# Delta rule in a streaming trunk: the first inverse correction from 16-bit copies, and the decay columns as the exponential's bias

## Chip, core and metric

The kernel runs on one core of a Trainium2 chip. The metric is the device time in microseconds of one execution. The core's engines are TensorE (PE in the profile; PEld is its weight load), VectorE (DVE), ScalarE (ACT), GpSimd (POOL) and SyncE (SP), which here issues all the DMAs.

## What is computed

One layer of a hybrid trunk, for a prompt of 2048 tokens and 64 further tokens of a running stream. Half of the mixing width is a gated delta rule with 4 heads of 128, the other half a multi-scale pool; both go through one output projection, and a SwiGLU FFN follows. The delta rule is evaluated in chunks. For one head and one chunk, cut to what matters here:

```
G     = cumsum(g)                                   # log decay
gamma = exp(where(lower_incl, G[:, None] - G[None, :], -inf))
Lm    = where(lower_strict, (k * beta) @ k.T * gamma, 0)
T     = inverse(eye + Lm)                           # triangular
u, w  = T @ (v * beta), T @ (k * beta * exp(G))
qk    = (q @ k.T) * gamma
v_new = u - w @ S;  o = (q * exp(G)) @ S + qk @ v_new
S     = S * exp(G[-1]) + (k * exp(G[-1] - G)).T @ v_new
```

The inputs are 32-bit; the large matrix products are made of split operands (a high and a low part) in a faster format.

## The kernel before, in words

**Order of the work.** The function hybrid_kernel does not call the engines. It calls a class Machine, which notes each operation with its operands, and issues all of them at the end, in an order that a list scheduler finds (issue, pick and run): per engine, the operation of the lowest rank that is ready. It knows costs of each operation and latencies between engines. On TensorE it keeps operations of three kinds: "r" (float32r, the dense products), "f" (32-bit) and "h" (16-bit); f and h go ahead of r when they are ready, and may be held for a moment (HOLD) while r goes on. Each engine then works through its own list in order. The order on an engine is thus a result of the operations and of the table of costs: a change of a few operations moves others.

**The stages.** First four blocks of 512 prompt tokens (block 0 has the 64 stream tokens too). A block j has: the norm (norm_apply), the input projection (project; tiles pp, from h and the weights wsp), the decay rows (rows), four heads (head_project, then a Head), four pool groups and, one block later, the output projection (out_proj; tiles pz). Then the FFN in three blocks of 704 tokens (gate_up, down, down_strassen), from about 970 us. The weights are 32-bit in memory and split into two float32r parts by ACT and DVE.

**rows** makes, for all heads of a block, the cumulated log decay: Ghl holds it by rows in a high and a low float32r part; a small matmul into the tile pc turns it into columns, one for each chunk and head, and ACT takes their exponential into EC.

**A front** (class Front, all) treats two chunks of 128 tokens of one head; there are 32 for the prompt and one (h is None) for the stream tokens. Its steps, each on the next engine:
- TensorE turns the keys (ptk), ACT scales them (ktl) and takes norms (kn).
- rowmm writes the row G, the same in all partitions, into the PSUM tile gb; ACT takes its exponential (EG, in the tile TV32).
- Into the same gb TensorE adds the mask (negm, 16-bit, 0 or -1e30) and, by negmm, minus the column G: two float32r matmuls with seln as the moving operand. ACT takes exp of all 256 columns at once: Gam is gamma for two chunks.
- GpSimd takes the identity off (U, in the tile Gst), TensorE makes the products gr, DVE multiplies: U is Lm plus the strict part's scale, Gam becomes qk.
- Seven levels double the block size of the inverse in 16 bits. Each has GpSimd's mask (Um), two matmuls py, ACT's copy Yt, four matmuls pt and DVE's difference (TV). The last writes 32 bits: T and V, the inverse and its transpose.
- Two Newton corrections in 32 bits: GpSimd makes F = I - T, TensorE pf = U T, DVE F = F - pf; then px0 = F V, T = V + px0 on DVE; then px1 = F T, X = V + px1.
- TensorE turns the values (ptv), ACT scales them (vtk).

A front's tiles are taken by slot (NLEV = 3), and its operations are ranked early (BOOST). Head.prompt then goes through the chunks in order: pk, rhs, vn, po and the new state Sp.

The lines that the change touches are in Front.negmm, Front.all and rows. Almost every operation is recorded at one line, 278, where issue calls the engine; so in the profile operations are known by their tiles. In these names digits that belong to buffers are left out: gb_p is the tile gb of a prompt's front.

Of the kernel before, what the change touches and what calls it, by code (L numbers as in the profile page):

```python
# [9 lines left out]
F16 = mybir.dt.float16  # L10
BF16 = mybir.dt.bfloat16
F32 = mybir.dt.float32
F32R = mybir.dt.float32r
AF = mybir.ActivationFunctionType
# [4 lines left out]
P = 128  # L19
# [3 lines left out]
DEC = 64  # L23
NTOK = SEQ + DEC
C = 128
NF = 22
EPS = 1e-6
NH = 4
# [9 lines left out]
SO = PB[0] + 3  # L38
# [315 lines left out]
def hybrid_kernel(ctx, tc, a, o):  # L354
    nc = machine = Machine(tc.nc)
    act = nc.scalar.activation
# [6 lines left out]
    def cost(n, dt):  # L363
        clock["pe"] += n * (1.67e-3 if dt == F32 else 0.427e-3) + 0.005

    def mm(out, lhsT, rhs, start, stop, **kw):
        nc.tensor.matmul(out, lhsT, rhs, start=start, stop=stop, **kw)
        n = 1
        for d in out.shape[1:]:
            n *= d  # L370
        cost(n, rhs.dtype)
# [55 lines left out]
    def pool(name, where=ctx, early=False, behind=False, **kw):  # L427
        return Pool(machine, where.enter_context(tc.tile_pool(name=name, bufs=1, **kw)), early, behind)
# [7 lines left out]
    cp1, gp = pool("cp1", p1, True), pool("gp", p1, True)  # L436
# [49 lines left out]
    for j in range(NBLK):  # L486
        win = [("win", m) for m in range(21)]
        at = 5 + 4 * OUT_AFTER
# [324 lines left out]
    B = Block(0)  # L813
# [5 lines left out]
    at = 0  # L819
# [18 lines left out]
    seln = cp1.tile([P, 4, 1], F32R, tag="seln", name="seln")  # L838
# [5 lines left out]
    negm = cp1.tile([P, P], BF16, tag="negm", name="negm")  # L844
    nc.vector.tensor_copy(negm, lm_f[:, 7])

    negm2 = cp1.tile([P, P], BF16, tag="negm2", name="negm2")
# [4 lines left out]
    idbf = cp1.tile([P, P], BF16, tag="idbf", name="idbf")  # L852
# [9 lines left out]
    def bc(t, nch, n):  # L862
        return t.unsqueeze(1).to_broadcast([t.shape[0], nch, n])
# [4 lines left out]
    class Front:  # L868
# [39 lines left out]
        def negmm(self, ps):  # L908

            G = self.B.Ghl  # L910
            if self.h is None:
                for h in range(NH):
                    mm(ps[:, h * DEC : (h + 1) * DEC], G[:, SO : SO + P], seln[:, h, :].to_broadcast([P, DEC]),
                       start=False, stop=False)
            else:
                for c in range(2):
                    at = self.off + c * C
                    mm(ps[:, c * C : (c + 1) * C], G[:, at : at + C], seln[:, self.h, :].to_broadcast([P, C]),
                       start=False, stop=c == 1, skip_group_check=True)

        def all(self):
            tag, chunk = self.tag, self.chunk
            two = lambda ps: ps[:, : 2 * C].rearrange("p (c n) -> p c n", n=C)
            gt = lambda shape, dt, t, bufs, n="": gp.tile(shape, dt, tag=t, name=f"{t.split('_')[0]}{n}_{tag}", bufs=bufs)
            slot = self.i % NLEV
            lev = lambda dt, t, n="", shape=[P, 2, C], bufs=1: gt(shape, dt, f"{t}_{slot}", bufs, n)
# [9 lines left out]
            for c in range(2):  # L936
# [8 lines left out]
            gb = self.ps(f"gb_{tag}")  # L945
# [5 lines left out]
            nc.gpsimd.tensor_copy(EL, EG.rearrange("p c n -> p (c n)").rearrange("p (e n) -> p e n", n=n)[:, :, n - 1 : n])  # L951
            Qd = self.Qd = gt([P, 2, C], F32, "Qd", NOUT)
            tt(Qd, self.Yqk[:, 0, self.off : self.off + 2 * C].rearrange("p (c n) -> p c n", n=C), EG, ALU.mult)
            dd = gb if self.h is not None else self.ps(f"dd_{tag}")
            mm(dd[:, : 2 * C], idbf, bc(negm2 if self.h is None else negm, 2, C), start=dd is not gb, stop=False,
               skip_group_check=dd is gb)
            self.negmm(dd)
            if dd is not gb:
                self.rowmm(dd, False)
            Gam = self.QKG = gt([P, 2, C], F32, "Gam", NOUT)  # L960
            act(Gam, two(dd), AF.Exp)
            U = lev(F32, "Gst")
            nc.gpsimd.tensor_tensor(out=U, in0=Gam, in1=bc(ident, 2, C), op=ALU.subtract)
            yield LAT_G
            ps = self.ps(f"gr_{tag}")
# [36 lines left out]
            T, V = TV32[:, 0], TV32[:, 1]  # L1002
            F = lev(F32, "F")
            nc.gpsimd.tensor_tensor(out=F, in0=bc(ident, 2, C), in1=T, op=ALU.subtract)
            pf = self.ps(f"pf_{tag}")
            for c in range(2):
                mm(pf[:, c * C : (c + 1) * C], U[:, c], T[:, c], start=True, stop=True)
            tt(F, F, two(pf), ALU.subtract)
            yield LAT_F
            px = self.ps(f"px0_{tag}")  # L1010
            for c in range(2):
                mm(px[:, c * C : (c + 1) * C], F[:, c], V[:, c], start=True, stop=True)
            tt(T, V, two(px), ALU.add)
            yield LAT_D
            yield self.before(NX, "used")
# [1 line left out]
            px = self.ps(f"px1_{tag}")  # L1017
# [119 lines left out]
    def rows(B, pab):  # L1137

        j, YW, nch = B.j, B.YW, B.nch
        Ghl = B.Ghl = gp.tile([P, SO + P], F32R, tag="Ghl", name=f"Ghl{j}", bufs=2)  # L1140
        EC = B.EC = gp.tile([P, 4, 12], F32, tag="EC", name=f"EC{j}", bufs=2)
# [29 lines left out]
        pc = psg(f"pc{j}")  # L1171
        for c, (lo, n) in enumerate(chunks):
            mm(pc[:n, c * 12 : c * 12 + 12], Rt[:, lo : lo + n], sel12, start=True, stop=True)
        act(EC[:, :nch, :], pc[:, : 12 * nch].rearrange("p (c t) -> p c t", t=12), AF.Exp)
        if B.dec:

            ECs = B.ECs = cp1.tile([P, 3, 2], F32, tag="ECs", name="ECs")
            for i in range(2):
                t = slice(i * DEC, (i + 1) * DEC)
# [173 lines left out]
    for j in range(NBLK):  # L1353
# [34 lines left out]
        prev, B = B, (nxt if nxt is not None else B)  # L1388
# [23 lines left out]
    for k in (4, 5, 6, 7, 0, 1, 2, 3):  # L1412
        t = wpool.tile([P, 512], F32, tag="xc", name=f"od{k}", bufs=XBUFS["xc"])
# [22 lines left out]
    for nm in FH[3:]:  # L1436
        t = f2.tile([P, 4, 2, N2], F32R, tag=f"h{nm}", name=f"hB{nm}")
# [172 lines left out]
    for op in order:  # L1610
        b = op[1]
        if op[0] == "gu":
            f = op[2]
# [6 lines left out]
            if plain(b, gi):  # L1620
                if f == groups[gi][0] or f == groups[gi][0] + 2:
                    two = opool.tile([P, 2, 2, TB2], F32R, tag="op", name=f"h3l{f}_{b}", bufs=2)
# [8 lines left out]
        else:  # L1631
            f0, G = groups[op[2]]
# [25 lines left out]
NY, NLEV, NOUT, NX = 3, 3, 3, 2  # L1658
# [128 lines left out]
```

## Time and profile before

| | |
|---|---|
| median of 3 runs | 2384.84 us (2381.84 to 2387.46) |
| the profiled execution | 2383.12 us |
| its span, first to last instruction | 2380.5 us |
| mean granted TensorE clock | 0.997 |
| DMA | 540.57 MB, mean 227 GB/s |

The time of an execution is a little more than the span, by 2.6 us here. A row of a timeline has its start, its length and the engine, then the tiles (written tile, arrow, read tiles), the shape and the number of instructions merged. Matmuls overlap, so a length is not what one costs; the distance between two starts is. A 32-bit matmul of the program leaves two records, a float32r or 16-bit one leaves one. Idle time stands in brackets or after a bar, with the engine that ended it.

### The profile page before, as it was taken

How to read it: one execution, taken by the hardware profiler on the slowest of the kernel's cores; microseconds unless marked ns; L12 is line 12 of the kernel's file. 1: busy time of each engine (PE TensorE's matmuls, PEld its weight loads, DVE VectorE, ACT ScalarE, POOL GpSimd, SP SyncE). 2: the span in 40 equal slices, each digit the busy share in tenths (PEclk: the TensorE clock that was granted, in tenths of full speed). 3: DMA queues.
4: the chain of work that ended last, by engine and by line, in shares of the span. 5: the costliest groups of instructions: out<-in, count | busy, mean ns of one | idle time of the engine just before them, and what ended most of it. 6: DMA issues, size and time to landing. Idle time of an engine off the chain costs nothing.

```text
span 2380.5 us, 41651 instructions
## 1 busy us (share of the span) xinstructions
PE 2344.3 (98%) x14823; PEld 2184.7 (92%) x14823; DVE 1674.3 (70%) x2943; ACT 1215.7 (51%) x2738; POOL 967.2 (41%) x1130
## 2 busy tenths in 40 slices
PE   9999999999999999999999999999999999999998
PEld 8999798777887778899999999999999999999998
DVE  7999875785577686787776883767566657646466
ACT  6666654564456565574454654553334554425334
POOL 1656452554346662264332536353233464202211
PEclk9999999999999999999999999999999999999999
DMA  7643566445555565998876678887855697565763
GB/s 267 224 165 134 189 228 217 146 165 190 176 182 172 162 195 166 311 373 324 312 282 240 257 270 271 295 287 248 283 189 175 201 348 247 193 227 193 260 209 114
DMA packets 228384, 540.57 MB, mean 227 GB/s; under 512 B 28240, under 2 KB 86608, under 8 KB 228176
## 3 DMA queue, kind: packets, MB, share of 16 engines
q1 hardware_dynamic: 228176, 537.92, 66.2%
q8 instruction: 116, 1.90, 0.3%
q14 instruction: 92, 0.75, 0.1%
HBM read 389.41 MB, written 148.41 MB: 226 GB/s over the span
## 4 chain that ended last, share of the span: by engine, by line
PE 81%; DVE 9%; ACT 3%; DMA 3%; issue 2%; SPq 1%; POOL 1%; DVEq 0%; POOLq 0%; ACTq 0%
PE px L278 19%; PE pp L278 14%; PE pz L278 11%; PE py L278 9%; PE d L278 8%; PE dx L278 5%; PE dy L278 3%; PE pk_p L278 2%; PE pt_p L278 1%; PE dz L278 1%; PE gr_p L278 1%; PE px_p L278 1%; DVE Yqk L278 1%; PE py_p L278 1%; ACT E L278 1%
## 5 line engine op out<-in xcount | busy, mean ns | idle before, releaser
L278 PE MATMUL pp<-h,wsp 128*128 128x512 f32 (+1 forms) x2480 | 562.1, 366 | 2.0 <-DVE h L278 1.7
L278 PEld LDWEIGHTS pp<-h,wsp 128*128 128x128 f32 x2480 | 402.3, 190 | 49.8 <-DVE h L278 2.6
L278 POOL TENSOR_TENSOR Um_p<-Gst_p,lmask 128x256 f16<-128x256 f32 x224 | 178.2, 809 | 109.6 <-PE py_p L278 80.9
L278 PE MATMUL pz<-op,wsp 128*128 128x512 f32 (+1 forms) x960 | 216.8, 366 | 3.4 <-ACT op L278 2.9
L278 PE MATMUL d<-h3l,wsd 128*128 128x352 f32 x1248 | 201.3, 322 | 0.2 <-DVE h3l L278 0.2
L278 PEld LDWEIGHTS d<-h3l,wsd 128*128 128x128 f32 x1248 | 199.1, 188 | 1.2 <-DVE h3l L278 0.7
L278 PEld LDWEIGHTS pz<-op,wsp 128*128 128x128 f32 x960 | 155.9, 190 | 23.2 <-ACT op L278 3.4
L278 DVE TENSOR_TENSOR TV_p<-TV_p,pt_p 128x512 f16<-128x512 f16 (+1 forms) x192 | 128.5, 681 | 48.7 <-PE pt_p L278 43.4
L278 PE MATMUL px<-hA,ws 128*128 128x352 f32 x792 | 141.2, 322 | 0.6 <-DMA ws<-g 0.6
L278 PE MATMUL pz<-hB,ws 128*128 128x352 f32 x792 | 139.6, 322 | 0.6 <-DMA ws<-g 0.6
L278 PE MATMUL px<-hBT,ws 128*128 128x352 f32 x792 | 137.8, 322 | 2.1 <-DVE u L278 2.1
L278 PE MATMUL px<-hBT,wsS 128*128 128x352 f32 x792 | 137.7, 322 | 2.0 <-ACT g L278 1.9
L278 PE MATMUL py<-hB,wsS 128*128 128x352 f32 x792 | 139.2, 322 | 0.1
L278 PE MATMUL px<-hA,wsS 128*128 128x352 f32 x792 | 137.4, 322 | 0.9 <-ACT g L278 0.9
L278 PE MATMUL py<-hA,wsS 128*128 128x352 f32 x792 | 137.1, 322 | 0.0
L278 ACT ACTIVATE hr<-g 128x352 f32<-128x352 f32 x132 | 65.6, 497 | 133.4 <-DVE g L278 133.4
L278 PEld LDWEIGHTS px<-hBT,wsS 128*128 128x128 f32 x792 | 128.2, 188 | 2.8 <-ACT g L278 2.8
L278 PEld LDWEIGHTS px<-hBT,ws 128*128 128x128 f32 x792 | 128.0, 188 | 2.9 <-DVE u L278 2.7
L278 PEld LDWEIGHTS px<-hA,ws 128*128 128x128 f32 x792 | 128.9, 188 | 1.0 <-DMA ws<-g 0.9
L278 PEld LDWEIGHTS pz<-hB,ws 128*128 128x128 f32 x792 | 128.6, 188 | 0.8 <-ACT hB L278 0.8
L278 PEld LDWEIGHTS px<-hA,wsS 128*128 128x128 f32 x792 | 128.3, 188 | 1.2 <-ACT g L278 1.1
L278 PEld LDWEIGHTS py<-hB,wsS 128*128 128x128 f32 x792 | 128.6, 188 | 0.4 <-ACT u L278 0.4
(686 smaller groups left out, 5354.5 us busy)
## 6 DMA issues: line engine op xcount, KB each, us to landing
wsS<-gS SPq DMA_DIRECT2D x176, 512.0 KB, 4.7
ws<-g SPq DMA_DIRECT2D x132, 512.0 KB, 4.6
wsp<-wnd SPq DMA_DIRECT2D x126, 512.0 KB, 3.3
gS<-wsS SPq DMA_DIRECT2D x88, 512.0 KB, 5.6
g<-ws SPq DMA_DIRECT2D x66, 512.0 KB, 5.5
wnd<-wsp SPq DMA_DIRECT2D x42, 512.0 KB, 4.5
xd<-x2d SPq DMA_DIRECT2D x96, 176.0 KB, 4.0
wrd<-in_wd_dram SPq DMA_DIRECT2D x48, 256.0 KB, 4.7
```

The costliest lines, as they stand in the source:

```text
L278: getattr(getattr(self.nc, op.eng), name)(*args, **kw)
```

## The change

The decay columns: negmm is left to the stream's front. A prompt's front now ends the group in gb with the mask, and ACT takes the exponential of each chunk alone, with minus the column G as its bias, one number for each partition. This column is a new tile NG, which rows writes from the same PSUM tile pc as EC, with factor -1.

The first correction: ACT copies V and F to a 16-bit tile VF (it takes the slot's buffer TV0, free by then; in the order it is called TV0w), and px0 is made from the copies by 16-bit matmuls. The second correction is still in 32 bits, from F and T.

```
         def negmm(self, ps):
 
             G = self.B.Ghl
-            if self.h is None:
-                for h in range(NH):
-                    mm(ps[:, h * DEC : (h + 1) * DEC], G[:, SO : SO + P], seln[:, h, :].to_broadcast([P, DEC]),
-                       start=False, stop=False)
-            else:
-                for c in range(2):
-                    at = self.off + c * C
-                    mm(ps[:, c * C : (c + 1) * C], G[:, at : at + C], seln[:, self.h, :].to_broadcast([P, C]),
-                       start=False, stop=c == 1, skip_group_check=True)
+            for h in range(NH):
+                mm(ps[:, h * DEC : (h + 1) * DEC], G[:, SO : SO + P], seln[:, h, :].to_broadcast([P, DEC]),
+                   start=False, stop=False)
...
-            dd = gb if self.h is not None else self.ps(f"dd_{tag}")
-            mm(dd[:, : 2 * C], idbf, bc(negm2 if self.h is None else negm, 2, C), start=dd is not gb, stop=False,
-               skip_group_check=dd is gb)
-            self.negmm(dd)
-            if dd is not gb:
+            Gam = self.QKG = gt([P, 2, C], F32, "Gam", NOUT)
+            if self.h is None:
+                dd = self.ps(f"dd_{tag}")
+                mm(dd[:, : 2 * C], idbf, bc(negm2, 2, C), start=True, stop=False)
+                self.negmm(dd)
                 self.rowmm(dd, False)
-            Gam = self.QKG = gt([P, 2, C], F32, "Gam", NOUT)
-            act(Gam, two(dd), AF.Exp)
+                act(Gam, two(dd), AF.Exp)
+            else:
+                mm(gb[:, : 2 * C], idbf, bc(negm, 2, C), start=False, stop=True, skip_group_check=True)
+                for c in range(2):
+                    act(Gam[:, c], two(gb)[:, c], AF.Exp, bias=self.B.NG[:, self.c0 + c, self.h : self.h + 1])
...
             tt(F, F, two(pf), ALU.subtract)
+            VF = lev(F16, "TV0", "w", [P, 2, 2, C])
+            nc.scalar.copy(VF[:, 0], V)
+            nc.scalar.copy(VF[:, 1], F)
             yield LAT_F
             px = self.ps(f"px0_{tag}")
             for c in range(2):
-                mm(px[:, c * C : (c + 1) * C], F[:, c], V[:, c], start=True, stop=True)
+                mm(px[:, c * C : (c + 1) * C], VF[:, 1, c], VF[:, 0, c], start=True, stop=True)
             tt(T, V, two(px), ALU.add)
...
-        act(EC[:, :nch, :], pc[:, : 12 * nch].rearrange("p (c t) -> p c t", t=12), AF.Exp)
+        pcs = pc[:, : 12 * nch].rearrange("p (c t) -> p c t", t=12)
+        act(EC[:, :nch, :], pcs, AF.Exp)
+        NG = B.NG = gp.tile([P, 4, NH], F32, tag="NG", name=f"NG{j}", bufs=2)
+        act(NG[:, :nch], pcs[:, :, :NH], AF.Copy, scale=-1.0)
```

Where instructions stand now is shown at three places. In the names p_3_1 is the second front of head 3 (of the block at hand); h_2 is the normed input of block 2, pp_20 an input projection's tile; a number at the end only tells buffers apart.

TensorE in the third block, where the last front's decay is made; before:

```order
L278 LDWEIGHTS idbf
L278 MATMUL gb_p_3_1_2175<-negm,idbf 128x256
L278 MATMUL pk_p_2_1_2171<-rhs_p_2_1_2172,X_p_2_1_2123 128x128
L278 MATMUL gb_p_3_1_2175<-seln,Ghl_1500 128x128 x2
L278 MATMUL pp_20_0_2049<-h_2_1444,wsp_79_1996 128x512 x4
```

The same place now:

```order
L278 LDWEIGHTS idbf
L278 MATMUL gb_p_3_1_2202<-negm,idbf 128x256
L278 MATMUL pk_p_2_1_2198<-rhs_p_2_1_2199,X_p_2_1_2149 128x128
L278 MATMUL pp_19_0_2072<-h_2_1459,wsp_78_2000 128x512 x5
L278 LDWEIGHTS TV_p_3_0_2164
```

The pair of seln between the 32-bit step pk and the dense matmuls is gone; the dense matmuls now follow pk itself.

TensorE in the second block, from pf to px0 of front p_3_0; before:

```order
L278 MATMUL pf_p_3_0_1536<-TV_p_3_0_1380,Gst_p_3_0_1385 128x128 x2
L278 MATMUL pp_20_0_1401<-h_1_774,wsp_50_1349 128x512 x7
L278 MATMUL px_p_3_0_1537<-TV_p_3_0_1380,F_p_3_0_1535 128x128 x2
L278 LDWEIGHTS Um_p_3_1_1575
L278 MATMUL py_p_3_1_1577<-TV_p_3_1_1554,Um_p_3_1_1575 128x128
```

The same place now:

```order
L278 MATMUL pf_p_3_0_1554<-TV_p_3_0_1395,Gst_p_3_0_1400 128x128 x2
L278 MATMUL pk_p_2_1_1558<-Sp,Yqk_2_1232 128x128
L278 MATMUL po_p_2__1500<-Qd_p_2_1_1331,Sp 128x128
L278 MATMUL pp_20_0_1414<-h_1_762,wsp_50_1363 128x512 x3
L278 MATMUL pp_19_0_1413<-h_1_763,wsp_49_1341 128x512 x4
L278 LDWEIGHTS TV0w_p_3_0_1555
L278 MATMUL px_p_3_0_1556<-TV0w_p_3_0_1555 128x128
```

Between pf and px0 there were seven dense matmuls, and there are seven and two steps of the preceding head; px0 reads only the copies.

ACT in the second block, around the copies of the same front; before:

```order
L278 ACTIVATE Gam_p_3_1_1528<-gb_p_3_1_1525 128x256
L278 CAST Yt_p_3_0_1499<-py_p_3_0_1498 128x256
L278 CAST op_1_1216<-pd_1_1405 128x512
L278 CAST Yt_p_3_0_1517<-py_p_3_0_1516 128x256
L278 ACTIVATE vn_p_2_1_1545<-pk_p_2_1_1539,kn_p_2_1_1310 128x128
L278 CAST Yt_p_3_1_1556<-py_p_3_1_1555 128x256
L278 CAST h_2_1444<-xb_1088_1446 128x512
```

The same place now:

```order
L278 CAST Yt_p_3_0_1535<-py_p_3_0_1534 128x256
L278 ACTIVATE Gam_p_3_1_1546<-gb_p_3_1_1543,NG_832 128x128 x2
L278 ACTIVATE vn_p_2_1_1552<-pk_p_2_1_1539,kn_p_2_1_1319 128x128
L278 CAST TV0w_p_3_0_1555<-TV_p_3_0_1395 128x256
L278 CAST TV0w_p_3_0_1555<-F_p_3_0_1553 128x256
L278 CAST h_2_1459<-xb_1088_1461 128x512
```

The exponential of the other front is in two parts with NG as an operand, and the two copies stand together ahead of the next block's h.

## Prediction

> **What bounds the kernel now.** I read the page first, then a table of the span cut into stages, then the waits of the TensorE, and last its timeline inside one stage. The page gives the span and the share of the busiest engine:
>
> ```profile
> span 2380.5 us, 41651 instructions
> ...
> PE 2344.3 (98%) x14823; PEld 2184.7 (92%) x14823; DVE 1674.3 (70%) x2943; ACT 1215.7 (51%) x2738; POOL 967.2 (41%) x1130
> ```
>
> The TensorE has 36 us without a matmul. All that the change touches runs in the four token blocks of the delta stage, before about 970 us. This is the table by stage; the first two numbers of a row are its ends and its length, and each engine's busy time follows with its count of instructions:
>
> ```profile
> core 0: us, PE busy (x) PEld busy (x) DVE busy (x) ACT busy (x) POOL busy (x), PEclk, DMA share, GB/s
> ...
> 60.00:245.00 185.00, 182.53 (x1491) 169.76 (x1490) 174.71 (x351) 117.58 (x302) 114.49 (x163) 1.00 0.53 179
> 245.00:480.00 235.00, 232.53 (x1514) 197.89 (x1515) 165.83 (x302) 128.40 (x315) 98.39 (x137) 1.00 0.57 192
> 480.00:715.00 235.00, 234.65 (x1397) 188.33 (x1397) 157.26 (x277) 122.67 (x306) 104.39 (x146) 1.00 0.53 178
> 715.00:970.00 255.00, 247.14 (x1464) 199.30 (x1463) 191.63 (x338) 143.12 (x358) 131.60 (x169) 0.99 0.57 177
> ...
> 1080.00:2381.00 1301.00, 1283.70 (x7992) 1275.84 (x7990) 855.20 (x1443) 591.84 (x1212) 459.84 (x446) 1.00 0.71 245
> ```
>
> Between 60 and 970 us the TensorE lacks 185+235+235+255 less 182.53+232.53+234.65+247.14, which is 13.2 us in 910. ACT is busy 52 to 64 per cent of each of these stages, DVE 67 to 94. The TensorE's waits on steps of the fronts (a front is the chain that inverts two chunks of one head) are short and few; the columns are the total, the number of waits and the longest:
>
> ```profile
> PE pt_p L278 <- ACT Yt_p L278: 1.4, 2, 0.9
> ...
> PE ptv_p L278 <- DVE X_p L278: 0.7, 1, 0.7
> PE py_p L278 <- DVE TV_p L278: 0.7, 2, 0.5
> ...
> PE px_p L278 <- DVE TV_p L278: 0.4, 1, 0.4
> ```
>
> 33 fronts with some twenty dependent steps each cost 3.2 us of waits in these four rows together. The dense matmuls (pp, the input projection; pz, the output projection) fill the time in which a front's step is on another engine. So in this stage time is what the TensorE has to issue, and a matmul taken from it is worth its distance to the next start, not its recorded duration (the records overlap). These are distances in the second block; a row is start, length, instructions:
>
> ```profile
> 437.81 0.29 PE L278 MATMUL py_p<-TV_p,Um_p 128*128 128x128 f16 x2
> 437.94 0.66 PE L278 MATMUL pf_p<-TV_p,Gst_p 128*128 128x128 f32 x4
> ...
> 439.39 0.28 PE L278 MATMUL gb_p<-negm,idbf 128*128 128x256 bf16 x1
> 439.51 0.28 PE L278 MATMUL pt_p<-Yt_p,TV_p 128*128 128x128 f16 x2
> 439.62 0.28 PE L278 MATMUL pt_p<-TV_p,Yt_p 128*128 128x128 f16 x2
> 439.71 0.41 PE L278 MATMUL gb_p<-seln,Ghl 128*128 128x128 f32 x2
> 439.96 0.45 PE L278 MATMUL pp<-h,wsp 128*128 128x512 f32 x1
> 440.24 0.61 PE L278 MATMUL px_p<-TV_p,F_p 128*128 128x128 f32 x4
> 440.69 1.04 PE L278 MATMUL gr_p<-Yqk 128*128 128x256 f32 x4
> 441.56 0.61 PE L278 MATMUL pf_p<-TV_p,Gst_p 128*128 128x128 f32 x4
> 442.01 0.61 PE L278 MATMUL px_p<-TV_p,F_p 128*128 128x128 f32 x4
> 442.37 1.87 PE L278 MATMUL pp<-h,wsp 128*128 128x512 f32 x7
> 444.09 0.28 PE L278 MATMUL py_p<-id,Um_p 128*128 128x128 f16 x2
> 444.21 0.66 PE L278 MATMUL px_p<-TV_p,F_p 128*128 128x128 f32 x4
> 444.71 0.38 PE L278 MATMUL ptv_p<-consts,Yvz 128*128 128x128 f32 x2
> ...
> 445.86 0.29 PE L278 MATMUL py_p<-TV_p,Um_p 128*128 128x128 f16 x2
> 445.98 0.66 PE L278 MATMUL px_p<-TV_p,F_p 128*128 128x128 f32 x4
> 446.48 0.39 PE L278 MATMUL pk_p<-rhs_p,X_p 128*128 128x128 f32 x2
> ```
>
> A step of two chunks in 32-bit (px, shown as x4, since such a matmul leaves two records) keeps the TensorE for 0.45, 0.36, 0.50 and 0.50 us, a mean of 0.45. The 16-bit step of the same size (py and pt, x2) keeps it for 0.13, 0.11, 0.09, 0.12 and 0.12, a mean of 0.11. The pair of column matmuls (seln) keeps it for 0.25. One price is hidden: what it costs to come back to the dense matmuls. Their pace when nothing interrupts is in these rows:
>
> ```profile
> 614.20 0.39 PE L278 MATMUL os_p__1942<-osh_p__1943,onesr 128*128 128x512 f32 x1
> 614.43 0.62 PE L278 MATMUL pp<-h,wsp 128*128 128x512 f32 x2
> 614.90 0.40 PE L278 MATMUL os_p__1942<-osl_p__1944,onesr 128*128 128x512 f32 x1
> 615.13 15.59 PE L278 MATMUL pp<-h,wsp 128*128 128x512 f32 x68
> 630.57 0.60 PE L278 MATMUL ptk_p<-consts,Yqk 128*128 128x128 f32 x4
> ```
>
> From 615.13 to 630.57 are 68 matmuls, 0.227 us each. The seven at 442.37, which follow a 32-bit step, take 1.72 where 7 x 0.227 is 1.59: 0.13 for the return. The two at 614.43, which follow a matmul of the same number format as theirs (float32r), take 0.47 where 0.45 is due: 0.02; the one at 439.96, after seln, also float32r, 0.28: 0.05.
>
> **The change, part by part.** *The first correction from 16-bit copies.* 33 fronts replace one 32-bit step by a 16-bit one: 33 x (0.45 - 0.11) = 11.2 us off the TensorE. By the extremes of the rows it is 33 x (0.36 - 0.13) = 7.6 to 33 x (0.50 - 0.09) = 13.5; I take the means, since the step falls beside both kinds of neighbours.
>
> The Trainium skill, page "TensorE: Matmul & The Clock Gate", section "Back-to-back issue gap", gives about 81 ns for each matmul with its weight load in a sustained stream of 128 columns. By it the 16-bit step would keep the TensorE for 0.16 us and the saving would be 33 x 0.29 = 9.6; the trace has 0.11 for just this shape, and that is used.
>
> *The column matmuls.* 32 fronts lose the pair of seln, 32 x 0.25 = 8.0 us. The mask (negm) stays and now ends the group; at 0.12 before another 16-bit step it is neither cheaper nor dearer.
>
> *The order of the TensorE.* The scheduler writes another order, and it interrupts the dense matmuls more often. Counted along both orders up to the first FFN matmul, the dense matmuls are resumed 401 times after a 32-bit or 16-bit step and 88 times after float32r before, and 456 and 66 times after. The pair of seln used to be a cheap way back, and pieces that stood in one group now stand apart. At 0.12 and 0.03 that is 55 x 0.12 - 22 x 0.03 = 6.0 us given back. Its bounds are nothing (if the gaps of the dense matmuls hide it) and 55 x 0.13 = 7.2.
>
> *ACT.* These rows price what ACT gets (busy time, then mean ns of one):
>
> ```profile
> L278 ACT ACTIVATE vn_p<-pk_p,kn_p 128x128 f32<-128x128 f32 x64 | 23.6, 368 | 45.8 <-PE pk_p L278 45.7
> ...
> L278 ACT ACTIVATE Gam_p<-gb_p 128x256 f32<-128x256 f32 x32 | 12.2, 385 | 1.6 <-PE gb_p L278 1.4
> ...
> L278 ACT CAST wsd<-wrd 128x256 fp32r<-128x256 f32 x24 | 9.7, 402 | 18.2 <-PE py L278 10.5 <-PE px L278 4.2 <-PE pz L278 3.5
> ```
>
> The copies are of the last kind: 66 x 0.40 = 26.5 us. The decay exponential becomes two of the first kind, with a column as an operand: 32 x (2 x 0.37 - 0.385) = 11.4. The negated column, once a block, is small: four at 0.37 at most, 1.5. Together 39 us, which takes ACT from 52-64 per cent of the stages to about 56-69. On the path to the end I cost it at nothing: the dense matmuls hide it. The front itself gets longer by one copy, 0.40 and a handover, so about 0.45 us from F to px0 (V's copy is done while pf runs); against that the exponential no longer waits for the seln pair. If the cover is gone in every front it costs 33 x 0.45 = 14.9 us, which is more than the gain; the four waits above say that cover is nearly always there.
>
> *Not touched.* No DMA, no DVE and no GpSimd instruction is added. The order of the TensorE from the first FFN blocks on is the same, so the 1301 us from 1080 us on stay, and shift.
>
> The sum: -11.2 - 8.0 + 6.0 = -13.2 us. The profiled execution took 2383.1, 1.7 under the median of the runs, 2384.84; the sum gives 2369.9 against the one and 2371.6 against the other. I predict 2371.
>
> **Rivals.** *The chain paces the stage, not the TensorE* (no change). For it: weight loads fill only 188.33 of the 235 us from 480 on, and DVE is at 94 per cent in the first block. The Trainium skill, page "Perfetto Trace Analysis", section "Identifying the Most-Contended Engine", calls matmul busy time a poor measure of headroom and takes the busy share of weight loads instead; by that rule there is a fifth of headroom in this stage and the removed matmuls would buy little. Against it: 0.35 us without a matmul in that stage, and dense matmuls at an even 0.227. Then what is saved turns into waits, and the time stays within 4.8 us of the median, 2380 to 2385. Chance 0.08.
>
> *ACT's queue stands* (slower). ACT works in order. The copy of F waits for the TensorE (pf) and DVE; four copies of the next block's h, vn and Yt are queued behind it, and the TensorE needs them. If the copy stands at the head too early by 1.0 us a front and the TensorE has nothing left to fill with, 33 us come on top: 2371 + 33 = 2404. It decides from 13.2/33 = 0.40 us a front for no gain, and from (13.2+4.8)/33 = 0.55 for slower by 0.2 per cent. Against it: the waits of Yt, same engine and same kind of place, reach the TensorE with 1.4 us in the whole run. Chance 0.05.
>
> *The weight load sets the pace of the 16-bit step* (a smaller gain). A weight load of this kind takes 98 ns:
>
> ```profile
> L278 PEld LDWEIGHTS <-TV_p x384: 95/98/102, 66.4 to 939.6; 128*128 128x128 f16 x192
> ```
>
> If it isn't hidden, the new step keeps the TensorE for 0.20 and not 0.11, 33 x 0.09 = 3.0 us less gain: 2374. The Trainium skill, page "TensorE: Matmul & The Clock Gate", section "LDWEIGHTS (loading the stationary operand)", gives columns / 1.2, so 107 ns, in the same direction. Against it: the rows of py and pt, with such loads, stand 0.09 to 0.13 apart. Chance 0.04, within the range.
>
> That the change does nothing is excluded by the order: seln is gone and the 16-bit step is there.
>
> **How the numbers follow.** The forecast has 0.83. Its best case is 13.5 + 8.0 with no price for returns, 21.5 us: 2361.6. Its worst has 7.6 + 8.0 - 7.2 = 8.4, and the copy's latency showing in a third of the fronts, 11 x 0.45 = 5.0: 3.4 left, 2379.7 against the profiled run and 2381.4 against the median. So the range is 2362 to 2381. About 0.2 per cent, 4.8 us, is what a measurement of this kernel can tell from no change, so faster means under 2380. Faster has 0.83 and 0.04 less a little for the worst case, 0.86; same 0.09; slower 0.05.
>
> **What would show it.** Right: no gb_p<-seln group; the 16-bit px step 0.09 to 0.13 us from the next start; the delta stage shorter by 10 to 16 us and the FFN stage equal; ACT up by about 39 us; waits of the TensorE on the new copies of a few us at most. Wrong: a row of TensorE waits on these copies, on Yt, h or wsp of more than 5 us; the delta stage as long as before with the TensorE less busy; or a new order with more returns than counted.

## The result, and the profile after

| | before | after |
|---|---|---|
| median | 2383.43 us (15 runs, 2380.63 to 2387.46) | 2378.36 us (15 runs, 2374.22 to 2382.42) |
| ratio to before, 95% interval | | 0.9976 [0.9968, 0.9984] |
| span of the profiled execution | 2380.5 us | 2376.5 us |
| mean granted TensorE clock | 0.997 | 0.995 |

The changed kernel is faster by 0.24%, 5.7 us by the ratio (the two medians lie 5.1 apart, the two profiled spans 4.0), where 13.2 were forecast: the right direction, less than half of the size. The page of the changed kernel, its span and engines:

```profile
span 2376.5 us, 41477 instructions
...
PE 2334.8 (98%) x14693; PEld 2168.0 (91%) x14693; DVE 1670.3 (70%) x2943; ACT 1245.3 (52%) x2840; POOL 967.8 (41%) x1130
```

The TensorE is 9.5 us less busy than the 2344.3 of before, yet the span is only 4.0 shorter. It now stands still for 41.7 us, where it was 36.2. The same table by stage as before:

```profile
60.00:245.00 185.00, 180.18 (x1454) 165.67 (x1452) 171.70 (x349) 124.79 (x327) 114.09 (x162) 0.99 0.53 180
245.00:480.00 235.00, 231.72 (x1498) 195.11 (x1499) 165.22 (x306) 137.16 (x343) 97.19 (x138) 1.00 0.58 194
480.00:715.00 235.00, 234.46 (x1400) 187.97 (x1399) 158.59 (x285) 131.62 (x333) 109.35 (x151) 1.00 0.54 181
715.00:970.00 255.00, 246.95 (x1427) 193.85 (x1426) 198.84 (x339) 153.94 (x389) 129.69 (x165) 0.99 0.60 187
```

Between 60 and 970 us the TensorE lacks 4.82 + 3.28 + 0.54 + 8.05 = 16.7 us, where it lacked 13.2. ACT's share of these stages rose to 56 to 67 per cent, where 56 to 69 were forecast; over the whole span ACT is busy 29.6 us more, not 39. What its new instructions cost, from the groups of ACT:

```profile
L278 ACT ACTIVATE Gam_p<-gb_p,NG 128x128 f32<-128x128 f32 x64 | 20.1, 375 | 1.8 <-PE gb_p L278 1.7
L278 ACT CAST TV0w_p<-F_p 128x256 f16<-128x256 f32 x32 | 13.1, 411 | 14.2 <-DVE F_p L278 14.0
L278 ACT CAST TV0w_p<-TV_p 128x256 f16<-128x256 f32 x32 | 13.0, 406 | 11.8 <-DVE TV_p L278 11.8
```

375 and 411 ns stand against 370 and 400 forecast. ACT's records overlap, and busy time counts an overlap once: the 64 exponentials are busy for 20.1 us, where 64 x 0.375 is 24.0. The new 16-bit step in the second block, from the timeline (start, length, instructions):

```profile
443.54 0.28 PE L278 MATMUL px_p<-TV0w_p 128*128 128x128 f16 x2
443.63 0.95 PE L278 MATMUL pp<-h,wsp 128*128 128x512 f32 x3
444.42 0.29 PE L278 MATMUL px_p<-TV0w_p 128*128 128x128 f16 x2
444.51 0.94 PE L278 MATMUL pp<-h,wsp 128*128 128x512 f32 x3
```

From its start to the next are 0.09 us in these two places. Over the 32 fronts of the prompt the mean is 0.11, as forecast. The weight load does not set its pace; that would be 0.20.

**Where the time went.** The table is worked out from the traces. For each matmul it takes the distance to the next one's start, without the time in which no matmul ran, sums it by kind up to the first FFN matmul (px from hA), and puts the time without a matmul in a column of its own. The levels are the 16-bit steps with the mask; float32r are the seln pairs, the norms and row sums; time at half clock is inside the kinds. The last column runs from the first FFN matmul to the end of the span. Each row is one profiled execution; that of e2 is 5.8 us over the median of its runs, the others lie within 2.

| kernel | dense | 32-bit steps | 16-bit px | float32r | levels | no matmul | FFN begins at | to the end |
|---|---|---|---|---|---|---|---|---|
| before | 705.8 | 169.5 | - | 33.5 | 70.3 | 16.3 | 996.5 | 1384.0 |
| after | 712.0 | 156.2 | 3.6 | 24.9 | 71.4 | 19.6 | 988.7 | 1387.8 |
| e1 columns | 704.0 | 169.7 | - | 25.2 | 70.3 | 16.7 | 987.1 | 1383.2 |
| e2 copies | 711.8 | 157.7 | 3.7 | 33.1 | 71.1 | 21.0 | 999.5 | 1390.8 |
| e6 F by DVE | 707.7 | 159.0 | 3.4 | 25.3 | 69.7 | 14.8 | 981.0 | 1382.9 |
| e8 hold | 703.1 | 157.2 | 3.5 | 24.9 | 70.4 | 14.9 | 975.0 | 1387.9 |
| e9 pools | 709.0 | 155.8 | 3.7 | 25.2 | 71.5 | 16.0 | 982.3 | 1383.1 |
| e13 hold and pools | 699.6 | 156.3 | 3.5 | 25.1 | 69.5 | 8.7 | 963.8 | 1385.9 |

After against before: the first correction -13.3 + 3.6 = -9.7, the columns -8.6, the dense matmuls with their returns +6.2. Those are the three terms of the forecast (-11.2, -8.0, +6.0). Then come three that it did not have: +1.1 in the levels, +3.3 without a matmul, and +3.8 in the FFN. Together they are 8.2 us.

Two places, the end of the delta stage and the start of the FFN, have longer waits than before. The waits of the TensorE in the changed kernel (total, number, longest):

```profile
PE px L278 <- ACT g L278: 5.3, 4, 2.7
PE py_p L278 <- DVE TV_p L278: 3.6, 5, 1.4
PE pz L278 <- ACT op L278: 3.0, 2, 2.3
```

And two of these rows before:

```profile
PE pz L278 <- ACT op L278: 2.9, 2, 2.2
PE px L278 <- ACT g L278: 2.7, 3, 1.4
```

The levels' py waited 0.7 on TV before and 3.6 now, so the four rows of waits that the prediction showed grew from 3.2 to 5.1 us. The copies needn't be the reason: in e1, which has none, py waits 2.8. The waits of pz on op are no longer in total than before, but they now stand elsewhere: the longest of before ended at 886 us, and there the changed kernel waits 2.15 us for DVE's wsp instead. The end of the delta stage, first before:

```profile
960.30 1.02 PE L278 MATMUL os_p__2961<-osq_p__2960,ones 128*128 128x512 f32 x2
960.75 8.76 PE L278 MATMUL pz<-op,wsp 128*128 128x512 f32 x35
969.68 27.03 PE L278 MATMUL pz<-op,wsp 128*128 128x512 f32 x118 [0.17 <-ACT wsp L278]
```

And the same place after:

```profile
951.96 1.02 PE L278 MATMUL os_p__2998<-osq_p__2997,ones 128*128 128x512 f32 x2
952.42 2.88 PE L278 MATMUL pz<-op,wsp 128*128 128x512 f32 x10
957.58 31.31 PE L278 MATMUL pz<-op,wsp 128*128 128x512 f32 x129 [2.28 <-ACT op L278]
```

os is the sum of squares with which the last head of the last block is normed. Its output op follows some 5 us later, and the rest of pz needs it. Before, 35 other pz were left to fill that time; now there are 10, and 2.28 us stand empty. The stock of dense work is fixed by now, and the order had used more of it between the earlier steps: 139 pz are left behind os, where 153 were.

The second place is the start of the FFN. The TensorE's timeline there, before:

```profile
1034.83 2.08 PE L278 MATMUL px<-hBT,ws 128*128 128x352 f32 x12
...
1038.66 2.08 PE L278 MATMUL py<-hA,wsS 128*128 128x352 f32 x12
...
1042.48 2.08 PE L278 MATMUL pz<-hB,ws 128*128 128x352 f32 x12
1045.10 2.20 PE L278 MATMUL px<-hBT,wsS 128*128 128x352 f32 x12 [0.53 <-ACT g L278]
```

ACT's, before:

```profile
1043.82 0.49 ACT L278 CAST h3l<-hr 128x352 fp32r<-128x352 f32 x1 [0.26 <-DVE hr L278]
1044.21 0.49 ACT L278 ACTIVATE sq7n<-xd 128x352 f32<-128x352 f32 x1
1044.61 0.43 ACT L278 COPY g<-px 128x352 f32<-128x352 f32 x1
```

The TensorE's, after:

```profile
1029.27 1.12 PE L278 MATMUL py<-hA,wsS 128*128 128x352 f32 x6
1031.22 2.18 PE L278 MATMUL px<-hBT,ws 128*128 128x352 f32 x12 [0.82 <-DVE u L278]
1033.24 1.12 PE L278 MATMUL py<-hA,wsS 128*128 128x352 f32 x6
...
1036.10 2.08 PE L278 MATMUL pz<-hB,ws 128*128 128x352 f32 x12
1040.84 3.74 PE L278 MATMUL px<-hBT,wsS 128*128 128x352 f32 x12 [2.66 <-ACT g L278]
```

ACT's, after:

```profile
1039.95 0.48 ACT L278 CAST h3l<-hr 128x352 fp32r<-128x352 f32 x1 [1.41 <-DVE hr L278]
1040.34 0.45 ACT L278 COPY g<-px 128x352 f32<-128x352 f32 x1
```

px needs the buffer that ACT's copy g empties. ACT works in order, and that copy stands behind h3l in both kernels. What differs is when h3l can start. Counted from the start of the last pz ahead of the wait, it was 1.34 us before and is 3.85 us now, and it waits 1.41 us for DVE's hr. The wait of px grew from 0.53 to 2.66. Why hr comes so late was not traced further. The order is a new one here on every engine: on the TensorE px from hBT and ws stood ahead of py from hA, and now stands between its two halves; ACT and DVE differ within their first 200 or so instructions of the FFN. From the first matmul of the down projection (d) on, the TensorE's order is the old one again.

Of the FFN's 3.8 us, 3.2 stand ahead of this d: from the first FFN matmul to it are 87.0 us, where there were 83.9, and from there to the end 1300.8, where there were 1300.1.

Both waits have a stretch at half clock beside them. Here is the row of the second for 20 us, with the granted clock behind POOL. It is 0.91, where before (the first row) has 1.00, and the twelve px above last 3.74 us where before's took 2.20:

```profile
1040.00:1060.00 20.00, 17.95 (x110) 17.16 (x109) 16.21 (x23) 15.07 (x34) 9.21 (x8) 1.00 0.99 363
...
1040.00:1060.00 20.00, 19.16 (x110) 19.16 (x111) 13.39 (x24) 15.68 (x33) 10.80 (x10) 0.91 0.90 336
```

### The profile page after: what moved, and what is told of

Its sections match the earlier page's. It is cut to its first block, busy times and chain, and to the rows that moved or that the text cites. A ratio compares the mean times of both kernels' runs of the same rounds, so it can differ in the third digit from the quotient of the medians.

```text
span 2376.5 us, 41477 instructions
## 1 busy us (share of the span) xinstructions
PE 2334.8 (98%) x14693; PEld 2168.0 (91%) x14693; DVE 1670.3 (70%) x2943; ACT 1245.3 (52%) x2840; POOL 967.8 (41%) x1130
## 4 chain that ended last, share of the span: by engine, by line
PE 53%; DVE 3%; DMA 2%; issue 1%; ACT 1%; SPq 0%; POOLq 0%; DVEq 0%; ACTq 0%
PE px L278 19%; PE py L278 9%; PE d L278 8%; PE pz L278 6%; PE dx L278 6%; PE dy L278 3%; PE dz L278 1%; DVE hr L278 1%; DVE hq L278 1%; DVE y L278 1%; DVE wsd L278 0%; DVE wsdS L278 0%; DMA out_yT_dram<-y 0%; DMA ws<-g 0%; DVE wsS L278 0%
## 5 line engine op out<-in xcount | busy, mean ns | idle before, releaser
L278 PE MATMUL pp<-h,wsp 128*128 128x512 f32 (+1 forms) x2480 | 569.4, 368 | 4.9 <-DMA wsp<-wnd 2.2
```

Of the source, the lines that this page charges most:

```text
L278: getattr(getattr(self.nc, op.eng), name)(*args, **kw)
```

## The experiments

The theories, in words. The sum's own: each microsecond taken from the TensorE counts, and local losses are set off. Its first rival: only a part (5.7/13.2 = 0.43) of any such saving passes on. The next: the copy of F, a step that the front didn't have, costs the rest; or ACT's load does. The last: each order that the scheduler finds has waits and half-clock stretches of its own, above all where the last head ends, and the forecast left those out. Ratios are to the kernel before, timed beside each run, with 95% intervals; a difference between two runs is taken from their ratios, unless times are given.

**e1, the columns alone.** The changed kernel, but px0 from F and V in 32 bits, without the copies:

```
-            VF = lev(F16, "TV0", "w", [P, 2, 2, C])
-            nc.scalar.copy(VF[:, 0], V)
-            nc.scalar.copy(VF[:, 1], F)
...
-                mm(px[:, c * C : (c + 1) * C], VF[:, 1, c], VF[:, 0, c], start=True, stop=True)
+                mm(px[:, c * C : (c + 1) * C], F[:, c], V[:, c], start=True, stop=True)
```

> The decay columns as the bias, the first correction still in 32 bits. Priced by start-to-start distances, the TensorE has 5.0 us less to issue (the seln pairs less the added returns to the dense matmuls). Theory A, every microsecond of the TensorE counts and what the full change lost was lost at single places of its own order: 5 us under the kernel before, ratio 0.998. Theory B, a chain or the DMAs of the transition to the FFN pace the stage and pass on about four tenths of what is saved: 2 us under, ratio 0.999. Theory C, each new order of the scheduler has its own waits and half-clock stretches, several us to either side: anywhere from 0 to 10 us under, and the profile shows the difference to 5.0 as waits of the TensorE and half-clock stretches.

0.9956 [0.9944, 0.9968], 2373.81 us. This half alone is faster than the whole. Both single figures, 0.998 and 0.999, lie outside the interval, and the result is at the edge of what the theory of orders allowed. float32r falls by 8.3 us, dense by 1.8, the time without a matmul rises by 0.4, and the FFN is 0.8 shorter.

**e2, the copies alone.** The kernel before, with the copies and the 16-bit px0, and with the seln pairs:

> The first correction from 16-bit copies, the decay columns still by seln. The TensorE has 8.5 us less to issue, ACT 26 us more. Theory A: ratio 0.9964. Theory B: 0.9985. Theory C: off 8.5 by several us, and the profile shows by what waits and half-clock stretches.

1.0006 [0.9996, 1.0016], 2386.3 us: nothing is left of a step that became 11.8 - 3.7 = 8.1 us cheaper. Theories A and B both missed. In the profiled execution, the slowest of its runs (2392.06), dense is 6.0 dearer, 4.7 more are without a matmul, and the FFN is 6.8 longer. Its tail:

```profile
961.82 1.02 PE L278 MATMUL os_p__2994<-osq_p__2993,ones 128*128 128x512 f32 x2
962.28 0.79 PE L278 MATMUL pz<-op,wsp 128*128 128x512 f32 x1
967.06 13.29 PE L278 MATMUL pz<-op,wsp 128*128 128x512 f32 x44 [3.99 <-ACT op L278]
```

The same wait as after, and worse: it had one pz left. The clock of these 20 us is 0.83:

```profile
960.00:980.00 20.00, 16.01 (x56) 11.98 (x55) 10.98 (x20) 8.77 (x17) 1.26 (x1) 0.83 0.73 229
```

**e3, the second correction from the copies too.** The changed kernel; px1 is the first product again, so the second correction's own product is left out:

```
-                mm(px[:, c * C : (c + 1) * C], F[:, c], T[:, c], start=True, stop=True)
+                mm(px[:, c * C : (c + 1) * C], VF[:, 1, c], VF[:, 0, c], start=True, stop=True)
```

> The full change with the second correction made from the same two 16-bit copies as the first (it repeats the first correction's product and so leaves out the second correction's own). No work is added on ACT; the TensorE has 23.7 us less to issue than before, 9.7 less than with the change. Theory A: a further 9.7 us under the changed kernel if its losses stay, ratio to before about 0.9935; 0.990 if they go. Theory B: 0.9958. Theory C: between 0.989 and 0.996.

0.992 [0.9908, 0.9932], 2364.25 us: 0.56 points less than after, 13 us for a step of 0.34 x 33 = 11.2. Theory B's 0.9958 lies outside the interval, so the rival of a fixed part falls. That all of the step passes on isn't shown: this is another order too, and in its trace the px are 10.3 us cheaper and the dense matmuls 5.7.

**e4, the first correction twice.** The kernel before with px0 made twice in 32 bits:

```
                 mm(px[:, c * C : (c + 1) * C], F[:, c], V[:, c], start=True, stop=True)
+                mm(px[:, c * C : (c + 1) * C], F[:, c], V[:, c], start=True, stop=True)
```

> The kernel before with the product of the first correction made twice (the second overwrites the first with the same values). The TensorE has 15.2 us more to issue. Theory A: ratio 1.0064. Theory B: 1.0025. Theory C: 1.004 to 1.009.

1.0044 [1.0032, 1.0056], 2394.21 us, +10.5. That is neither theory A's 1.0064 nor B's 1.0025. The profiled execution has 14.6 us more in 32-bit steps (184.1 against 169.5; 33 x 0.45 is 14.9) and 3.7 less without a matmul. The price of the step is confirmed, and a gap took up a part.

**e5, copies that nobody reads.** The kernel before with ACT's two copies, px0 as before:

> The kernel before with ACT's two copies of V and F made in each front but read by nobody: the first correction stays in 32 bits. The TensorE's issue is priced as before (0.1 us more). Theory D, the copy costs as a step in the front's path (F, copy, first correction): nobody waits for it here, so no change, ratio 0.999 to 1.001. Theory E, the copies cost as load on ACT, which works in order and delays what stands behind: the 8 to 10 us that the copies alone lost against their price come here too, ratio 1.003 to 1.004. Theory C, luck of each order: anything within 5 us.

0.9982 [0.9973, 0.9991], 2380.77 us. The copies, which make ACT busy for 20.7 us more (26 by their mean durations), cost nothing in this order, and the time is even a little shorter than theory D allowed. ACT's load alone isn't the cause.

**e6, F in 16 bits straight from DVE.** The changed kernel; DVE subtracts twice from the same PSUM tile, and ACT copies V only:

```
-            tt(F, F, two(pf), ALU.subtract)
...
-            nc.scalar.copy(VF[:, 1], F)
+            tt(VF[:, 1], F, two(pf), ALU.subtract)
+            tt(F, F, two(pf), ALU.subtract)
```

> The full change, but DVE writes the 16-bit F straight from the PSUM tile, before the 32-bit one (one more DVE instruction of 0.41 us in a front), and ACT copies only V. The TensorE's issue is priced 13.7 us under the kernel before. Theory D: the step is out of the path, so most of the price is kept, 11 to 14 us under, ratio 0.994 to 0.9955. Theory E: half of the copies' load is gone, ratio 0.996. Theory C: anything between 0.993 and 0.999.

0.9922 [0.9909, 0.9936], 2366.79 us, 0.54 points less than after and less than any of the theories gave. It seems to speak for the copy as the cause. But its trace has no wait at the tail, dense is 4.3 cheaper, and the FFN is 4.9 shorter, where no copy stands. The order was another one. e14 and e15 take this up.

**e7 and e8, another order of the same operations.** In the kernel before (e7) and in the changed one (e8) the dense work may be held a little longer by the scheduler:

```
-HOLD = 0.4, 3.0
+HOLD = 0.5, 3.0
```

> The kernel before with the same operations in another order: the scheduler's first hold goes from 0.4 to 0.5. The TensorE's issue is priced 1.6 us less (368 returns to the dense matmuls after other formats, not 401). Theory A: ratio 0.9993. Theory C: the new order has its own waits and half-clock stretches; up to 5 us to either side of that.

> The changed kernel with the first hold at 0.5: the same operations as the changed kernel in another order, 15.1 us under the kernel before by the TensorE's price (404 returns). Theory C: what the changed kernel lost belongs to its order, so this one may come out at 8 to 15 us under. Theories D and E: the loss of about 8 us stays, 6 to 8 us under, ratio 0.997.

e7: 1.0014 [1.0005, 1.0023], 2388.03 us. e8: 0.9914 [0.9902, 0.9927], 2364.8 us. No engine's instructions differ in kind or count, and the changed kernel is 14.8 us faster, the one before 3.3 slower; e8 went beyond the 8 to 15 us under before that theory C gave. What an order costs is thus as large as the whole change. In e8 the dense matmuls are resumed 401 times after a 32-bit or 16-bit step and not 453 (up to the first FFN matmul), and dense falls by 8.9 us (2.3 of them are less half clock). Its tail still waits:

```profile
937.69 1.12 PE L278 MATMUL os_p__2998<-osq_p__2997,ones 128*128 128x512 f32 x2
943.02 17.15 PE L278 MATMUL pz<-op,wsp 128*128 128x512 f32 x63 [4.22 <-ACT op L278]
```

So does e7's, though it is the kernel before, with none of the changed operations:

```profile
964.99 1.11 PE L278 MATMUL os_p__2961<-osq_p__2960,ones 128*128 128x512 f32 x2
970.32 4.37 PE L278 MATMUL pz<-op,wsp 128*128 128x512 f32 x11 [4.22 <-ACT op L278]
```

**e9 and e10, the last head earlier.** In the last block the pools come after the third head and not after the second, in the changed kernel (e9) and in the one before (e10). Dense work is so left for the time after the last head:

```
-            plan += win[:9] + win[17:] + win[9:17]
+            plan += win[:13] + win[17:] + win[13:17]
...
-            if h == 1 and nxt is None:
+            if h == 2 and nxt is None:
```

> The changed kernel with one thing moved: in the last block the four pool groups are projected after the third head's projection instead of after the second's, so the last head's chain starts at the same place but the third's earlier, with the same operations (TensorE priced 15.1 us under the kernel before). Theory F, the last block's chain of heads ends later than the dense work that covers it, and the TensorE stands 2 to 4 us there and again, with half-clock stretches, at the start of the FFN: the chain ends earlier against the dense work, these waits go, and 5 to 9 us come back against the changed kernel, ratio to before 0.9935 to 0.996. Theory C in its plain form (luck of each order everywhere): anything between 0.992 and 0.999.

> The kernel before with the same move. Its TensorE has no wait at the end of the delta stage to be removed. Theory F: no more than 2 us of gain, ratio 0.999 to 1.000. Theory C: up to 5 us to either side.

e9: 0.9936 [0.9924, 0.9948], 2368.48 us. e10: 0.9992 [0.9984, 1.0001], 2382.27 us. Where the tail waits, the move gains 9.5 us; in the order of before, where it doesn't, nothing that can be told. The tail in e9 has no wait, and the dense matmuls run through (the view starts at 940 us; 213 pz follow os in all):

```profile
939.64 42.78 PE L278 MATMUL pz<-op,wsp 128*128 128x512 f32 x188
982.26 2.08 PE L278 MATMUL px<-hA,ws 128*128 128x352 f32 x12
```

The FFN is 4.7 us shorter too, with no wait of px on g over 1.4. The waits of the tail and of the FFN's start and their half-clock stretches went together.

**e11, keep the TensorE warm at the tail.** The changed kernel with two more 32-bit matmuls after the last head's os, whose result nobody reads:

```
+            if seqs[-1] is self and self.B.j == NBLK - 1:
+                for _ in range(2):
+                    mm(ps[:, :W], ones, osq[:, :W], start=True, stop=True)
```

> The changed kernel with two 32-bit matmuls of 512 columns more (written to a PSUM tile that nobody reads any more), at the place where the TensorE stands 2.3 us at the end of the delta stage, and the rest of its order the same. They keep the TensorE busy while it waits. If that wait sets off the half-clock stretch behind it, the stretch goes, 1.7 us less, ratio to before 0.997; if the stretch comes from something else, no change, 0.9976; if the two matmuls delay the dense work, up to 1 us more, 0.998.

0.9987 [0.9978, 0.9995], 2381.23 us: no gain; of the three figures only 0.998, that of a delay, lies in the interval. It didn't make its condition:

```profile
952.84 1.02 PE L278 MATMUL os_p__2998<-osq_p__2997,ones 128*128 128x512 f32 x2
953.30 2.88 PE L278 MATMUL pz<-op,wsp 128*128 128x512 f32 x10
956.09 1.98 PE L278 MATMUL os_p__2998<-osq_p__2997,ones 128*128 128x512 f32 x4
960.12 5.21 PE L278 MATMUL pz<-op,wsp 128*128 128x512 f32 x14 [2.05 <-ACT op L278]
```

The added matmuls ran for 2 us, and the pz that need op went on 7.3 us after os, where it had been 5.6 in the changed kernel. The wait stayed. What the half clock alone costs at the tail is left open.

**e12, the changed kernel again, a second profiled execution.**

> The changed kernel once more, for a second profile of the same order. Waits that the order sets (1.2 us near 88, 2.3 at the end of the delta stage, 2.7 at the start of the FFN) stand again within 0.3 us; the half-clock stretches, if they hang on where a wait falls in the clock gate's own windows, are other ones, and the two executions differ by these, 1.7 us each.

2381.45 us, span 2379.5, clock 0.992. The waits that were named are the same (1.21 us at 88, 2.28 at the tail, 2.63 at the FFN's start), so they belong to the order. Others aren't: 1.42 us at 718.7 became 2.70 at 720.3, and 1.24 at 396.7 is gone. Nor are the half-clock stretches: behind the first 50 us, 3.4 us at 88.6, 720.1, 959.0 and 1040.9 us in the first execution; 6.8 us at 246.3 and 720.7 and 3.4 at 870.9, 963.1 and 1045.0 in this one.

**e13, hold and pools together.** The changed kernel with the edits of e8 and e9:

> The changed kernel with a dense hold of 0.5 us and, in the last block, the pools after the third head: both edits that gained when made alone (0.9914 and 0.9936 of the kernel before). With the hold alone the last head's output was still waited for with 4.2 us and the FFN began with a further 2.6 us of waiting. Theory of the tail: an earlier start of the last head takes both waits away and 5 to 7 us go, so 0.9885 to 0.9895 of the kernel before, no wait over 0.9 us between 940 and 1060 us. Rival, each order has its own waits and one removed returns elsewhere: 0.9905 to 0.9935, with waits of another place in the trace.

0.9861 [0.9848, 0.9875], 2351.8 us: the fastest here, 26.6 us under the changed kernel, 13 under e8. Its page:

```profile
span 2349.7 us, 41499 instructions
...
PE 2320.2 (99%) x14693; PEld 2168.5 (92%) x14693; DVE 1662.3 (71%) x2943; ACT 1243.5 (53%) x2840; POOL 975.7 (42%) x1130
```

Its tail, with 177 pz after os and no stop:

```profile
922.76 1.02 PE L278 MATMUL os_p__2998<-osq_p__2997,ones 128*128 128x512 f32 x2
923.22 40.73 PE L278 MATMUL pz<-op,wsp 128*128 128x512 f32 x177
963.78 1.45 PE L278 MATMUL px<-hA,ws 128*128 128x352 f32 x8
```

The theory of the tail expected 5 to 7 us against e8 and is right in direction; the gain is about twice that, and a wait of 1.79 us is left at the FFN's start, where it allowed none over 0.9. 8.7 us are without a matmul up to the FFN, the least of all, and dense, at 699.6, is cheapest. Those go beyond the tail, and neither theory had them.

**e14, F by DVE and the pools moved.** The edits of e6 and e9:

> The changed kernel with DVE writing the 16-bit F, and in the last block the pools after the third head. With the DVE write alone (0.9922) nothing waited for the last head's output. Theory of the tail: the move has nothing to take away here and gains under 2 us, 0.9914 to 0.9926, while on the changed kernel itself it gained 0.0040. Rival, the move is worth something in itself with this change, whether or not the tail waits: it gains 0.003 to 0.005 again, 0.987 to 0.989.

0.9925 [0.9912, 0.9939], 2367.47 us, against 0.9922 of e6: the move gains nothing where no tail wait is left. That is what the theory of the tail says, and inside its figures.

**e15, all three.** The edits of e6, e8 and e9:

> All three edits on the changed kernel: DVE writes the 16-bit F, dense hold 0.5 us, pools of the last block after the third head. Theory of terms that add: the hold's fewer returns (6 us less issue than in the changed kernel) come on top of the tail without waits, 0.9885 to 0.990. Rival, each order has its own waits: anywhere from 0.990 to 0.995, and the trace shows new waits of 3 us or more or more half-clock stretches than the 3.4 us of before's.

0.9925 [0.9913, 0.9937], 2367.3 us. The terms don't add. The time is in the rival's range, but the rival's sign isn't in the trace: no wait of 3 us, and no more half clock than before. Against e13 it only has DVE's write in place of the copy of F, a shorter front, and is 15.5 us slower: 5.3 more without a matmul, 3.3 more dense, 2.4 more in 32-bit steps, and the rest in the levels and the FFN. So the copy of F as a step in the path isn't the cause either. Removing it gained 12.9 us in one order (after to e6), 2.6 in a second (e9 to e14, within the intervals) and lost 15.5 in a third (e13 to e15).

## Why the prediction was right or wrong

**The first correction: right.** -9.7 us against -11.2; its range was 7.6 to 13.5. A new step keeps the TensorE for 0.11 us, or 3.6 in all. The 9.7 contain all 32-bit steps; the px of the prompt's fronts alone fell by 10.9.

**The columns: right.** -8.6 against -8.0, and -8.3 when made alone (e1). The columns alone are worth 0.44%, nearly twice the whole change.

**The returns to the dense matmuls: right in kind, and the size in part by luck.** +6.2 against +6.0. While the clock was halved (half of the time counted as lost) the dense matmuls lost 6.6 us here and 4.5 before, so about 4.1 are left for the returns, 0.07 for each of the 55. In e8 against after, 52 returns fewer are worth 8.9 - 2.3 = 6.6 us, 0.13 each.

**ACT's time: near, and at nothing on the path.** ACT is busy 29.6 us more, not 39. e5 shows that the load of the copies is free in one order. That the copy as a step is free isn't shown for every front, but e13 and e15 show that it isn't what was lost.

**What failed: the waits were taken over from the order before.** "On the path to the end I cost it at nothing: the dense matmuls hide it" took it that the cover stays as the four rows of waits showed it. The sum was made for the TensorE's own work, at waits of the old order, and had no term for what a new order does between the last head and the FFN. Cut by place, the profiled execution shows what that step left out. Up to the last head's os the changed kernel is 8.3 us ahead and has 14 more of the last pz done, at 0.227 each: 11.5 us saved, of 13.2. From os to the first d it then loses 6.9 us. From there to the end it loses 0.7, so "the 1301 us from 1080 us on stay" came true; what failed is the stretch ahead of 1080, which no sentence priced. There 10 pz and not 35 are left to cover the last head's norm, and the copy g that px needs waits for a late hr.

By kind, the terms that the sum lacked are +3.3 us without a matmul, +3.8 in the FFN and +1.1 in the levels: 8.2 us in all, while the three forecast terms themselves came to -12.1.

**What shows it.** Take the stretch from the last head's os to the first d, less 0.227 us for each pz in it. Before has 85.4 us, after 92.2. In the seven traces whose pz wait 2 us or more for the last head's op (after, e2, e3, e7, e8, e11, e12) it is 89.8 to 95.2; in the ten others 83.5 to 86.9. e7, of the kernel before, is among the seven, so the loss belongs to an order and not to the changed operations. The move of the pools was made in four orders: where the tail waited it gained 9.5 us (after to e9) and 12.6 (e8 to e13), where it didn't 1.9 (before to e10) and -0.7 (e6 to e14), both within the intervals. The move also leaves another order elsewhere, so the whole of a gain can't be put down to the tail. That the tail's wait brings the FFN's start with it is a pattern, not a shown cause: px waits 2.62 to 2.66 us on g there in all seven, and 0 to 1.9 in the ten others, e13 with 1.79 among them.

**The rivals.** None of the three came. The chain paces the stage: no, 11.5 of the 13.2 us came off up to the last head. ACT's queue stands: not at the copies, which no wait of the TensorE in the changed kernel names, but the same mechanism did occur, at the FFN's start. The weight load: no. A fourth was missing: the change is a draw of a new order. Over the seven orders measured of the changed arithmetic (after, e6, e8, e9, e13, e14, e15) the ratios run from 0.9861 to 0.9976, with a mean of 0.992, 18 us; the three of the kernel before lie between 0.9992 and 1.0014. The changed kernel as it stands is the slowest of its seven, and the forecast of 13.2 us lies within them. They are no random sample: e6, e9 and what was made from them were picked to remove a loss.

**Left open.** Why hr comes late at the FFN's start wherever the tail waits, why the order of e13 wastes so little, and why e15 with the same two edits and a shorter front doesn't, was not settled. The returns alone (395 and 400) don't tell them apart.

## What to carry to other kernels

Where a scheduler sets the order, cost a change in two parts: the work that it takes off the busiest engine, which rows of the trace price well, and the waits of the new order, which the trace of the old one can't show. Compare the new order of every engine, not only of the busiest, at the places where a latency-bound chain ends a stage, and count the independent work that is left behind its last step. Before judging such a change by one run, time it in two or three orders; here they lie further apart than the change is worth.

## What the runs showed of the hardware

Stretches at half clock last 3.413 us or twice that, and begin about where the TensorE had stood for as little as 1.2 us (1.22 us at 87.6 us, stretch at 88.6), while a wait of 2.15 us at 881.1 in the same execution brought none. Which waits bring one differs between two executions of one order (e12). The Trainium skill, page "TensorE: Matmul & The Clock Gate", section "What's actually happening", has a free-running window of 3413 ns and half speed after an idle one; the length and the changing place agree with the traces, but waits of well under one window are enough here.

A wait of the TensorE can thus cost more than its length: up to half of the stretch on top, 1.5 us for the twelve px at 1040.84 (3.74 against 2.20).
